# A hybrid S5 / RWKV-7 / Hawk trunk on one core: two weight strips of the first projection in turns, and VectorE's first tile of x ahead of the S5 parameters

## The chip, the core and the metric

The kernel runs on one core of a Trainium2 chip. The metric is the device time of one execution in microseconds (us). Five engines of the core matter here: PE (TensorE, the matmuls), ACT (ScalarE), DVE (VectorE), POOL (GpSimd) and SP (SyncE, which starts most transfers). Each runs its own list of instructions in the order in which the program was built, and waits on semaphores for what the others produce. That order is fixed when the kernel is built; nothing is reordered on the chip.

## The reference

There is one sequence of 256 tokens of width 2048, and two layers, each a mixer followed by a dense SwiGLU network. The change touches only the first layer's mixer:

```
h = rms_norm(x, g)                       # x * rsqrt(mean(x*x) + eps) * g
p = h @ w_in                             # 2048 -> u (1024), r, k, v (3 x 1024), low-rank columns (288)
u -> S5: dt = exp(log_dt); abar = exp(lam * dt); bb = gamma(abar, lam) * b
     s[t] = abar * s[t-1] + bb @ u[t]    # complex diagonal recurrence, 64 groups x 64 modes
     y = gelu(Re(c @ s) + d * u);  y * sigmoid(y @ w_glu)
r, k, v, low-rank -> RWKV-7: a recurrence over t with a 64 x 64 state per head, 16 heads,
     a norm per head, a bonus and a gate
x = x + rms_norm(concat(y_s5, y_rw) @ w_out, g2)
```

Behind it come the network of layer 0, a Hawk block (gate, convolution, real recurrence) and the network of layer 1. All inputs, weights and outputs are 32-bit floats.

## The kernel before

**Matrix products.** Activations are held transposed, 128 features by 256 tokens to a tile (a k-tile). A weight matrix is cut into strips of up to 512 output columns and a strip into groups g of 256 rows, two k-tiles each. A group goes through three steps: SP fetches it as `raw` (512 KB; a ring of three buffers), ACT writes its rounded part `hi` (line 136), and DVE writes the rest, `lo` = raw - hi (line 112); `hi` and `lo` are rings of three too. x is split in the same way into `hh` (ACT) and `hl` (DVE). PE then computes hi·hh, hi·hl and lo·hh (lines 513, 514 and 515) for each k-tile and each 128 columns: 24 matmuls for a group of 512 columns. These are called strip matmuls below and are counted from the start of the kernel: W192 is the point behind the 192nd.

**Strips.** The list `groups`, filled by `plan(...)`, says in which order groups are fetched; a `Strip` object takes them in that order (`take`, `run`, `go`), and when its last group is through (`done`) its result in PSUM (`psw`) is evacuated. The u projection has two strips of 8 groups: u0 (W1 to W192), then u1 (W193 to W384). Then come the low-rank strip (8 groups of 18 matmuls, to W528) and eight strips for r, k and v (to W1680), two for w_glu (to W1872), and the output projection in two halves (to W2256 and W2640).

**The norm.** The strips run on x·g without the factor rsqrt(mean). Meanwhile ACT squares x (`sqs`), PE sums the squares (`ssq`), DVE works out the root (`rs`), PE spreads it over the partitions (`rstdp`), and the evacuation of each u strip multiplies `psw` by `rstd` on DVE (`normed`). The evacuation `u_evac(s)` then copies the strip into tiles `U`, half on ACT and half on DVE, 16 copies each.

**Side work.** While PE runs strips, generators in named lanes emit the S5 and RWKV work between strip matmuls. The lanes are paced by a clock model at build time (`L.now`, `clk`, `rdy`), which settles where each instruction lands in its engine's list. `params()` (lane "par") is the chain of small DVE operations from `lam` (lambda, log dt) to the powers `apr`/`api` and the matrix `bb`. The S5 block runs in eight entries e of 8 channel groups; for each, POOL and DVE write the tables `wb` and `cb` (via `n`) and the angle `ang`, ACT takes its sine `st` and cosine `ct`, PE transposes (`tp`), forms `kt` and `tm`, multiplies `bu` = U·wts, DVE runs the recurrence (`m`, `bu`, scan, `spr`, `spi`), PE sums `py`, and ACT's gelu writes `yg`. Entries 0 to 3 read U of strip u0, entries 4 to 7 that of u1. The tables have two buffers, `ang` and `kt` one, and entry e is not prepared before entry e-2 has been emitted to its end. RWKV runs over four parts hf: `elem`, `solve(hf)` (31 steps, partly on POOL), `chunks(hf)`, and `norm`, whose last steps (`tp`, `yl`, `gp`, `yrf`, `yrh`, `yrl`) make the input of the second half of the output projection.

**Start.** `some(14)` emits 14 steps of `params()` before anything else of this layer; then u0's first group calls `h_before(0)`, which makes the first group's `hi` and `lo` (`ready(1)`), then `hh` of four k-tiles, then `hl` of four.

## Time and profile before

| what | us |
|---|---|
| time, median of 3 runs | 2435.07 |
| lowest and highest run | 2434.27, 2438.75 |
| the profiled execution's own time | 2434.1 |
| its span (first to last instruction of the profile) | 2432.3 |
| PE busy in the span | 2358.0 |
| the first layer's mixer up to the end of its last strip (W2640) | 551.8 |

The span is what the trace shows; 1.8 us of the execution lie outside it. Matmuls overlap each other, so a matmul "lasts" 0.28 us in the rows and the next one starts 0.12 us later. The stage that the change touches lies in the first 551.8 us; what follows is the same code in both kernels.

### The profile page before, as it was taken

Reading aid. Unit: us, or ns where it says so; the run is one execution under the profiler, and the core shown is the slowest. Engines: PE = TensorE matmul, PEld = TensorE weight load, DVE = VectorE, ACT = ScalarE, POOL = GpSimd, SP = SyncE. Lnnn points to the kernel's source line nnn. Section 1 sums busy time; section 2 is a strip of 40 time slices with the busy share of each in tenths; the row PEclk is TensorE's granted clock in tenths of the full one; section 3 lists DMA queues with packets and bytes.
Section 4 is the critical chain, followed back from the end, with each engine's and each line's share of the span. In section 5 each row is a group of like instructions: output and inputs, shape, how many; then the busy total and the mean of one; then the engine's idle time right before and its main releaser. Section 6 shows DMA issues by size and latency. Waiting matters only on the chain.

```text
span 2432.3 us, 47365 instructions
## 1 busy us (share of the span) xinstructions
PE 2358.0 (97%) x19830; PEld 2313.1 (95%) x19830; DVE 1457.4 (60%) x2002; ACT 1180.8 (49%) x1550; POOL 410.5 (17%) x589
## 2 busy tenths in 40 slices
PE   7888999998999999999999999998999999999997
PEld 7888888998999999999999899998999999999997
DVE  9786667568655544555544877757555544555544
ACT  5566545445444444444443687945444444444443
POOL 4773665515000000000000400014000000000002
PEclk8899999999999999999999999999999999999999
DMA  5222534454555555555554455564555555555553
GB/s 199 65 87 83 157 111 134 122 176 148 182 184 185 185 184 184 185 182 186 182 183 164 156 179 194 173 195 137 185 182 187 182 187 186 183 182 183 185 187 114
DMA packets 127446, 404.21 MB, mean 166 GB/s; under 512 B 26112, under 2 KB 26880, under 8 KB 127104
## 3 DMA queue, kind: packets, MB, share of 16 engines
q1 hardware_dynamic: 126912, 399.61, 50.1%
q8 instruction: 155, 2.54, 0.4%
q0 software_dynamic: 320, 1.58, 0.2%
q14 instruction: 59, 0.48, 0.1%
HBM read 397.98 MB, written 3.15 MB: 165 GB/s over the span
## 4 chain that ended last, share of the span: by engine, by line
PE 74%; DVE 3%; POOL 1%; ACT 1%; issue 1%; POOLq 0%; ACTq 0%; DVEq 0%
PE psw L513 24%; PE psw L515 24%; PE psw L514 24%; DVE lo L112 1%; DVE xl L131 1%; POOL xr L112 1%; ACT hi L136 0%; PE ssq L263 0%; PE warm L263 0%; PE own L515 0%; PE own L514 0%; PE own L513 0%; POOL sqs L112 0%; DVE sqs L112 0%; POOL tg L112 0%
## 5 line engine op out<-in xcount | busy, mean ns | idle before, releaser
L112 DVE TENSOR_TENSOR lo<-raw,hi 128x1024 fp32r<-128x1024 f32 (+1 forms) x760 | 931.6, 1230 | 868.9 <-ACT hi L136 867.2
L136 ACT ACTIVATE hi<-raw 128x1024 fp32r<-128x1024 f32 (+1 forms) x760 | 783.7, 1035 | 931.6 <-PE psw L514 733.1
L514 PE MATMUL psw<-xl,hi 128*128 128x256 f32 x3328 | 943.3, 283 | 15.1 <-DVE xl L131 14.8
L513 PE MATMUL psw<-xh,hi 128*128 128x256 f32 x3328 | 942.5, 283 | 0.9 <-ACT xh L136 0.9
L515 PE MATMUL psw<-xh,lo 128*128 128x256 f32 x3328 | 941.4, 283 | 0.0
L514 PEld LDWEIGHTS psw<-xl,hi 128*128 128x128 f32 x3328 | 635.9, 191 | 19.8 <-DVE xl L131 19.8
L513 PEld LDWEIGHTS psw<-xh,hi 128*128 128x128 f32 x3328 | 635.9, 191 | 1.5 <-ACT xh L136 1.5
L515 PEld LDWEIGHTS psw<-xh,lo 128*128 128x128 f32 x3328 | 636.2, 191 | 0.0
L515 PE MATMUL psw<-hhi,lo 128*128 128x256 f32 x1364 | 384.8, 282 | 0.0
L513 PE MATMUL psw<-hhi,hi 128*128 128x256 f32 x1364 | 384.8, 282 | 0.0
L514 PE MATMUL psw<-hlo,hi 128*128 128x256 f32 x1364 | 384.3, 282 | 0.0
L112 POOL TENSOR_TENSOR sqs<-sqs 128x512 f32<-128x512 f32 x44 | 73.0, 1659 | 1519.2 <-ACT sqs L136 1518.7
L514 PEld LDWEIGHTS psw<-hlo,hi 128*128 128x128 f32 x1364 | 257.9, 189 | 0.0
L513 PEld LDWEIGHTS psw<-hhi,hi 128*128 128x128 f32 x1364 | 257.9, 189 | 0.0
L515 PEld LDWEIGHTS psw<-hhi,lo 128*128 128x128 f32 x1364 | 257.9, 189 | 0.0
L513 PE MATMUL psw<-hh,hi 128*128 128x256 f32 x560 | 173.7, 310 | 4.8 <-ACT hi L136 3.2
L514 PE MATMUL psw<-hl,hi 128*128 128x256 f32 x560 | 164.2, 293 | 5.4 <-DVE hl L131 5.4
L515 PE MATMUL psw<-hh,lo 128*128 128x256 f32 x560 | 164.5, 294 | 4.0 <-DVE lo L112 3.9
L513 PEld LDWEIGHTS psw<-hh,hi 128*128 128x128 f32 x560 | 111.1, 198 | 12.7 <-issue 5.8
L514 PEld LDWEIGHTS psw<-hl,hi 128*128 128x128 f32 x560 | 111.6, 199 | 6.3 <-DVE hl L131 6.0
L515 PEld LDWEIGHTS psw<-hh,lo 128*128 128x128 f32 x560 | 111.3, 199 | 5.7 <-DVE lo L112 5.5
L136 ACT ACTIVATE ga<-ga 128x512 f32<-128x512 f32 x52 | 32.8, 632 | 83.0 <-DVE ga L112 82.9
(424 smaller groups left out, 2719.9 us busy)
## 6 DMA issues: line engine op xcount, KB each, us to landing
raw<-in_w_fg SPq DMA_DIRECT2D x352, 512.0 KB, 3.5
raw<-in_w_fd SPq DMA_DIRECT2D x176, 512.0 KB, 3.5
raw<-in_w_oi SPq DMA_DIRECT2D x64, 512.0 KB, 4.0
raw<-in_w_p SPq DMA_DIRECT2D x64, 384.0 KB, 3.2
raw<-in_w_eo SPq DMA_DIRECT2D x32, 512.0 KB, 3.6
raw<-in_w_oo SPq DMA_DIRECT2D x32, 512.0 KB, 3.7
raw<-in_w_u SPq DMA_DIRECT2D x16, 512.0 KB, 4.4
raw<-in_w_glu SPq DMA_DIRECT2D x8, 512.0 KB, 3.5
```

The lines of the kernel that those rows point to most:

```text
L112: e.tensor_tensor(o, x, y, op=op)
L131: e.scalar_tensor_tensor(o, x, s, y, op0=op0, op1=op1)
L136: S.activation(o, x, f, bias=bias, scale=scale)
L513: TE.matmul(o, hi[:, kk, sl], xh, start=st, stop=False, skip_group_check=True)
L514: TE.matmul(o, hi[:, kk, sl], xl, start=False, stop=False, skip_group_check=True)
L515: TE.matmul(o, lo[:, kk, sl], xh, start=False, stop=en, skip_group_check=True)
```

## The change

Three edits. The 16 groups of the two u strips are planned and run in the order of a table `TURNS`, so that both strips stand open in PSUM at once and a k-tile of x serves both before the next is needed. `some(14)` goes, so that all steps of `params()` are emitted by the lane "par"; and `h_before(0)` makes `hh` and `hl` of the first k-tile before the first weight group is split. `solve(hf)` of hf 2 and 3 starts to be emitted only when `chunks(hf-2)` has been emitted to its end.

```diff
+        def strips_in_turns(a, b):
+            for z, g in TURNS:
+                (a, b)[z].go(g)
...
+        TURNS = [(0, 0), (1, 0), (0, 1), (1, 1), (0, 2), (1, 2), (0, 3), (1, 3), (0, 4), (0, 5), (1, 4),
+                 (0, 6), (1, 5), (0, 7), (1, 6), (1, 7)]
+
+        def plan_two(a, b):
+            for z, g in TURNS:
+                plan(((a, b)[z], range(g, g + 1)))
...
-        plan(*w_u, w_lr, *w_p, *w_glu, *w_eo[0], (w_eo[1][0], range(3)), (w_eo[1][1], range(3)),
+        plan_two(*w_u)
+        plan(w_lr, *w_p, *w_glu, *w_eo[0], (w_eo[1][0], range(3)), (w_eo[1][1], range(3)),
...
-            def some(n):
-                for _ in range(n):
-                    next(par)
...
             keep_warm(10)
-            some(14)
...
                 if g == 0:
+                    h_high(0)
+                    h_low(0)
                     ready(1)
+                    ks = ks[1:]
                 for k in ks:
                     h_high(k)
...
-            vdone, ndone = set(), set()
+            vdone, ndone, cdone = set(), set(), set()
...
-                while "ready" not in H:
+                while "ready" not in H or hf > 1 and hf - 2 not in cdone:
                     yield 0.5
...
                     L.add("gn", norm(hf, c2, yc, ys, vr, rs))
+                cdone.add(hf)
...
-            strip(w_u[0], hx, W4, u_evac(0), mid=(h_before, h_behind, hat.get))
-            strip(w_u[1], hx, W4, u_evac(1))
+            strips_in_turns(Strip(w_u[0], hx, W4, u_evac(0), mid=(h_before, h_behind, hat.get)),
+                            Strip(w_u[1], hx, W4, u_evac(1)))
```

Three places show how this moves instructions. The first is DVE's list at the start of the kernel, before the change, from the first parameter row to the first of x; `en` to `y` are rows of `params()`.

```order
L120 TENSOR_SCALAR en<-lam 128x32
L118 TENSOR_SCALAR en<-en 128x32
...
L120 TENSOR_SCALAR y_144<-y_142 128x32
L120 TENSOR_SCALAR omu<-vec 128x27
...
L112 TENSOR_TENSOR lo<-raw,hi 128x1024
L131 SCALAR_TENSOR_TENSOR hl_120<-x0a,vec,hh_118 128x256 x4
L112 TENSOR_TENSOR lo<-raw,hi 128x1024
```

And the same place after it.

```order
L120 TENSOR_SCALAR omu<-vec 128x27
...
L131 SCALAR_TENSOR_TENSOR hl_120<-x0a,vec,hh_118 128x256
L112 TENSOR_TENSOR lo<-raw,hi 128x1024
L131 SCALAR_TENSOR_TENSOR hl_120<-x0a,vec,hh_118 128x256 x3
L112 TENSOR_TENSOR lo<-raw,hi 128x1024
L120 TENSOR_SCALAR en<-lam 128x32
L118 TENSOR_SCALAR en<-en 128x32
```

The parameters have gone behind the second `lo`, and one `hl` stands ahead of the first. The second place is ACT's list around the first gelu (`yg` of entry 0), before the change; `st` and `ct` are the sine and cosine of entry 1, and the `U` copies are the evacuation of strip u1.

```order
L136 ACTIVATE st<-ang 128x256
L136 ACTIVATE ct<-ang 128x256
L136 ACTIVATE ct<-ct 128x256
L136 ACTIVATE Tm_193<-tm 128x512
L136 ACTIVATE hi<-raw 128x576 x2
L136 ACT_TABLE_LOAD
L136 ACTIVATE yg<-py 32x256 x4
L136 ACTIVATE nn<-ang,cc__106 128x256
L136 ACTIVATE nn<-nn,cc__106 128x256
L136 ACTIVATE U_179<-psw_679 32x128 x4
```

And the same place after it, from the second strip's copies on.

```order
L136 ACTIVATE Tm_157<-tm 128x512
L136 ACTIVATE U_143<-psw_189 32x128 x4
...
L136 ACTIVATE U_146<-psw_189 32x128 x4
L136 ACTIVATE hi<-raw 128x576 x3
L136 ACTIVATE st<-ang 128x256
L136 ACTIVATE ct<-ang 128x256
L136 ACTIVATE ct<-ct 128x256
L136 ACT_TABLE_LOAD
L136 ACTIVATE yg<-py 32x256 x4
```

Strip u1's copies have come ahead of the sines of entry 1, which stood ahead of the first gelu and of those copies before. The third place is PE's list at the end of the RWKV part, where the last normalised tile goes through `tp` and `gp` and the next half of the output projection starts with `psw0` on new `hi`; before the change:

```order
L270 MATMUL tp_6556<-cst_75,yc_6450 128x128 x2
L513 MATMUL psw0_6471<-yrh_6301,hi_6473 128x256
...
L263 MATMUL gp_6567<-sg_221,g2_6284 128x128 x4
L513 MATMUL psw1_6472<-yrh_6301,hi_6473 128x256
...
L515 MATMUL psw1_6472<-yrh_6301,lo_6474 128x256
L263 MATMUL ssq_6601<-ones_76 128x1 x2
L513 MATMUL psw0_6303<-yrh_6301,hi_6516 128x256
```

And after it.

```order
L515 MATMUL psw1_6430<-yrh_6236,lo_6432 128x256
L270 MATMUL tp_6577<-cst_75,yc_6521 128x128 x2
L263 MATMUL gp_6582<-sg_185,g2_6358 128x128 x4
L263 MATMUL ssq_6601<-ones_76 128x1 x2
L513 MATMUL psw0_6238<-yrh_6236,hi_6489 128x256
```

Between `tp` and the strip matmul on the new `hi` there stood 21 strip matmuls (6 up to `gp`, 15 behind it); now there is none. In strip matmuls, the first `py` (entry 0) moves from W372 to W420, the second from W414 to W462, the third from W510 to W546, and the eighth stays at W888; `tp` of the last RWKV tile moves from W2379 to W2400.

## Rows read from the trace of the kernel before

**Rows 1.** The page, part 1: busy us (share of the span), instructions, by engine

```profile
PE 2358.0 (97%) x19830; PEld 2313.1 (95%) x19830; DVE 1457.4 (60%) x2002; ACT 1180.8 (49%) x1550; POOL 410.5 (17%) x589
```

**Rows 2.** Waits of PE in 0 to 552 us: waiter, releaser: total, times, longest

```profile
PE psw L514 <- DVE hl L131: 5.4, 3, 3.5
PE kt L263 <- POOL cb L112: 5.3, 4, 2.2
...
PE rstdp L263 <- DVE rs L131: 2.9, 1, 2.9
```

**Rows 3.** Windows by stage: length, busy us (instructions) of PE, PEld, DVE, ACT, POOL, PEclk, DMA

```profile
0.00:46.90 46.90, 33.80 (x224) 32.61 (x225) 41.66 (x132) 23.26 (x40) 13.67 (x26) 0.88 0.65 228
46.90:98.30 51.40, 45.05 (x360) 42.40 (x359) 41.09 (x77) 24.41 (x50) 43.85 (x49) 0.87 0.23 70
...
143.00:226.30 83.30, 70.56 (x573) 64.78 (x573) 65.72 (x133) 59.59 (x99) 40.92 (x50) 0.98 0.28 85
...
300.00:551.80 251.80, 248.99 (x2354) 227.84 (x2354) 162.66 (x335) 124.83 (x214) 116.10 (x241) 1.00 0.44 138
```

**Rows 4.** Windows, one stretch of low granted clock, same columns

```profile
46.20:49.60 3.40, 3.40 (x16) 3.40 (x17) 3.40 (x5) 0.39 (x1) 3.32 (x4) 0.51 0.00 0
```

**Rows 5.** Timeline of ACT at the start: start, length, operation [idle before, releaser]

```profile
6.06 1.06 ACT L136 ACTIVATE hi<-raw 128x1024 fp32r<-128x1024 f32 x1 [3.83 <-DMA raw<-in_w_u]
7.03 1.87 ACT L136 ACTIVATE hh<-x0a,vec 128x256 fp32r<-128x256 f32 x4
```

**Rows 6.** Timeline of DVE at the start

```profile
2.50 3.98 DVE L120 TENSOR_SCALAR en<-lam 128x32 f32<-128x32 f32 x1 [1.37 <-DMA lam<-in_s5lam]
...
9.81 1.22 DVE L112 TENSOR_TENSOR lo<-raw,hi 128x1024 fp32r<-128x1024 f32 x1
...
10.95 1.67 DVE L131 SCALAR_TENSOR_TENSOR hl<-x0a,vec,hh 128x256 fp32r<-128x256 f32 x4
```

**Rows 7.** Timeline of PE in strip u0

```profile
11.48 0.58 PE L514 MATMUL psw<-hl,hi 128*128 128x256 f32 x1 [3.53 <-DVE hl L131]
...
42.85 0.28 PE L514 MATMUL psw<-hl,hi 128*128 128x256 f32 x1
42.97 0.28 PE L515 MATMUL psw<-hh,lo 128*128 128x256 f32 x1
```

**Rows 8.** Timeline of DVE: first row of one entry's recurrence, and strip u1's scaling

```profile
91.91 0.75 DVE L112 TENSOR_TENSOR m<-st,bu 128x256 f32<-128x256 f32 x2 [3.62 <-PE bu L263]
...
98.25 1.29 DVE L112 TENSOR_TENSOR psw<-psw,rstd 128x512 f32<-128x512 f32 x2
```

**Rows 9.** Timeline of PE: first `py` of entries 0 and 7

```profile
86.95 0.33 PE L263 MATMUL py<-U,Tm 128*128 128x64 f32 x2
...
226.28 0.33 PE L263 MATMUL py<-U,Tm 128*128 128x64 f32 x2
```

**Rows 10.** Timeline of ACT from 80 to 112 us

```profile
80.36 0.40 ACT L136 ACTIVATE st<-ang 128x256 f32<-128x256 f32 x1
...
98.98 4.46 ACT L136 ACTIVATE U<-psw 32x128 f32<-32x128 f32 x16 [5.88 <-DVE psw L112]
...
109.85 1.28 ACT L136 ACT_TABLE_LOAD   x1
111.14 0.42 ACT L136 ACTIVATE st<-ang 128x256 f32<-128x256 f32 x1
```

**Rows 11.** Timeline of POOL from 81 to 95 us: entry 2's angle and last table

```profile
81.20 0.61 POOL L112 TENSOR_TENSOR ang<-cst,y 128x256 f32<-128x256 f32 x1 [1.96 <-ACT ct L136]
...
93.01 1.80 POOL L112 TENSOR_TENSOR cb<-n,n 64x320 f32<-64x320 f32 x2
```

**Rows 12.** Timeline of PE at the end of the RWKV part

```profile
523.82 0.38 PE L270 MATMUL tp<-cst,yc 128*128 128x128 f32 x2
...
524.75 1.63 PE L263 MATMUL gp<-sg,g 128*128 128x128 f32 x8
```

**Rows 13.** Timeline of DVE at the end of the RWKV part

```profile
527.56 0.76 DVE L112 TENSOR_TENSOR yrl<-yrf,yrh 128x256 fp32r<-128x256 f32 x2 [0.48 <-ACT yrh L136]
```

## The prediction

> **What bounds the kernel now.** The page's first part is read first: PE is busy 97% of the span, DVE 60%, ACT 49%, POOL 17% [rows 1]. PE sets the time, so a change can only shorten it where PE idles or runs slowly. The windows by stage show where that is: in the last 252 us of the mixer PE is idle for 2.8 us (251.80 less 248.99), but in 0 to 46.9 us for 13.1, in 46.9 to 98.3 for 6.35, and in 143 to 226.3 for 12.7 [rows 3]. The waits of PE name the releasers: `hl` 5.4 us in three waits, `cb` from POOL 5.3 in four, the root of the norm 2.9 in one [rows 2]. A second loss comes on top: after the 2.9 us wait, from 46.2 to 49.6 us, the granted clock is 0.51, that is the 1.2 GHz level, though PE is busy in all of it [rows 4]. At 0.51, 3.4 us do the work of about 1.7, so such a wait costs its own length and 1.7 more. Other long waits of this stage are followed by such a stretch too; I call the 1.7 a clock tax.
>
> At full clock a strip matmul follows the last after 0.12 us [rows 7]. Strip u0's 192 would need 23.0 us and take from 7.6 to 43.3: the strip is paced by its input.
>
> **The change part by part.**
>
> *Start.* Before, DVE begins with parameters: `en` at 2.50 holds it for 3.98 us (waiting within the instruction), and the first `lo` starts only at 9.81, the first `hl` at 10.95 [rows 6], though `hi` is done at 6.06+1.06 = 7.12 [rows 5]. PE waits 3.53 us for `hl` until 11.48 [rows 7]. After, ACT does one `hh` first (1.87/4 = 0.47 us), then `hi` (1.06), and DVE one `hl` (1.67/4 = 0.42), then `lo` (1.22). `hh` shows no wait for x at 7.03, so x is there by then; if it is there at 6.8, `hh` ends at 7.3, `hi` at 8.3, `lo` at 9.6. Before, the first `lo` matmul had its `lo` at 11.03 and ran behind `hl` at 11.86. So PE gets going about 2 us earlier. Bounds: 1.0 us if x lands late enough that `hh` starts at 8, and 3.5 if the whole wait goes. I take 2.0. The parameters now go behind the second `lo`. They have cover as long as `bb`, which the tables of entry 0 need, is not late. If that cover goes, they cost what DVE spent on them ahead of `lo`, 9.81 less 6.5 (where `en` ends) = 3.3 us [rows 6].
>
> *Turns.* A group of x tiles now serves 48 matmuls (5.76 us) instead of 24 (2.88 us), so x is wanted at half the rate. The waits for `hl` after the first (5.4 - 3.5 = 1.9 us, [rows 2]) lose their cause, and the 2.9 for the root too, since PE now has strip matmuls to run while DVE works the root out. That is 4.8 us, with two clock taxes 8.2. Against it stands the supply of weights: the strip's 16 groups must still be fetched and split, with x's tiles on the same two engines, and DVE is busy 41.66 of 46.9 us [rows 3]. Walking ACT, DVE and PE by the durations above, W192 is done near 35 instead of 43.3, but PE waits about 2.3 us for `lo` of group 11 (DVE is in the chain of the root then) and about 3.3 for `kt`, because `cb` of entry 0 is done only near 57.4. Strip u0 is complete at W336 instead of W192. Its evacuation, 1.29 us for both halves of `psw` [rows 8] and some 4.5 of copies (as ACT's, [rows 10]), starts at about 67, and two `lo` come next on DVE. Then `bu`, the recurrence (91.91 to 98.25, 6.3 us of DVE, [rows 8]) and `py` of entry 0 at 82 to 84 us, at W420. Before, it was at 86.95 [rows 9], at W372. The walk's times are estimates, added up from these durations. So PE is ahead by 48 × 0.12 = 5.8 us of strip work and about 4 us of time: a lead of 9.7 us. That is the gross gain of both edits together, the start's 2.0 in it.
>
> *What the lead runs into.* By the two orders of ACT, the sines of entry 1 stand before the first gelu and before u1's copies; afterwards they stand behind u1's copies (4.46 us, [rows 10]) and three `hi`. Before, `st` of entry 1 began at 80.36 [rows 10]; by the walk it begins at about 91. POOL's `ang` of entry 2 has one buffer and follows those sines (81.20 before, released by ACT's `ct`, [rows 11]): about 91.5. From there to the end of the last `cb` POOL took 94.8 - 81.2 = 13.6 us before [rows 11]. In the walk DVE takes some of these rows, and they end at about 102 instead of 94.8. PE, ahead of before, then waits for `kt` of entry 2 some 6 us, after another 5.6 for `lo` of the low-rank strip, which stands behind u1's evacuation on DVE. The lead at the second `py` is then about 3.4 us. After that DVE and POOL are ahead, since u1's evacuation is past, and the old waits of 143 to 226 us (12.7 us, [rows 3]) shrink; but between the first and the eighth `py` there are 468 strip matmuls instead of 516, 5.8 us less of cover. Carrying this through entry 7 I get a lead of 4 to 10 us at its `py` (226.28 before, [rows 9], same place W888). I take 7.0. Its low end is the second `py`'s lead; its high end the whole 9.7.
>
> *Three more table loads on ACT.* One is 1.28 us and the next activation starts 0.01 us after it [rows 10]. All three are 3.8 us of ACT, which is half idle, and one of them lies on the path to a gelu; it is inside the 7.0. The Trainium skill (ScalarE: Activation LUTs, What ACT_TABLE_LOAD costs) gives about 1283 ns for the load and 1380 ns of drain with it, 2.66 us for every switch to another set. By that, the three would be 8.0 us of ACT, and the sum up to 4.1 us worse if all three lay on the path, about no change in all. The trace agrees with the load and shows no drain behind it.
>
> *The gate on `solve`.* It moves solves 2 and 3 later; `qp` of part 3 goes from W1818 to W1938. In 300 to 551.8 us PE idles 2.8 us in all, so there is little to win, and POOL (116 of 252 us) and DVE (163) have room [rows 3]. The loss is at the end: `tp` of the last tile moves to W2400, and the strip matmul behind it needs its result. From `tp` at 523.82 [rows 12] to the end of `yrl` at 527.56+0.76 = 528.32 [rows 13] is 4.5 us. Before, 21 strip matmuls (2.5 us) and `gp` (about 1.55 us net, [rows 12]) covered all but nothing of it; now `gp` and `ssq` (about 2.3 us with their own fill) are the cover. 2.2 us of PE idle are left, plus 0.5 if `tp` itself comes late. Bounds: 0.5 if the chain is faster without strips beside it, and 5.0 with a late `yc` and a clock tax. I take 2.0.
>
> *Sum.* 7.0 won, 2.0 lost: 5.0 us off the profiled execution's 2434.1 is 2429.1. Its time is 1.0 below the median of the runs, which would give 2430.1; I say 2429.6. From the ends (3.4 won and 5.0 lost; 9.7 won and 0.5 lost): 1.6 us slower to 9.2 us faster, and a clock tax more or less at three places is 5 us either way: 2420 to 2440.
>
> **The rivals.**
>
> *The side chains take the lead back* (2435). The entries are made one after the other: `ang`, tables, `kt`, `bu`, recurrence. Where their chain is what PE waits for, being early at W420 only means waiting longer. For it: the `cb` and `kt` waits of the stage [rows 2], and the late sines. Against it: DVE is idle 10 of 51 us and 17.6 of 83 in two of the stages that follow [rows 3], so the chain isn't solid. A switch of ACT's table that held it longer than its row would lead to the same place: at twice 1.28 us [rows 10] three switches are 3.8 us later, 2433.4. The 0.01 us in [rows 10] speaks against it; it has 0.03 of this rival's chance. Otherwise the lead at entry 7 is 2 and the end costs 2: no change. The drain that the Trainium skill tells of (ScalarE: Activation LUTs, What ACT_TABLE_LOAD costs) would be such a longer hold.
>
> *Slower* (2441). One mechanism: with the sines of e1 behind u1's copies the two-deep tables lose one step of lead, and every entry up to 7 has its tables late; PE idles 12 us more from 85 to 226 and pays the tax at two places more. That is 9.7 - 12 - 3.4 - 2 = 7.7 us slower. It decides when entry 7's `py` comes later than 226.3. Against it: the fault is a single delay of about 10 us, and POOL has 42 of 83 us free [rows 3].
>
> *The lead is kept* (2424). The low-rank strip, at W385 to W528, is enough cover for the tables, and one or two clock taxes fall away: 9.7 + 1.7 won, 1.0 lost, from 2434.1.
>
> *The change doesn't do what it says.* Input, not order, paces strip u0, so turns only move the wait from x to weights: then only the start's 2.0 remain and the end eats it, 2434 to 2435. It is counted with the first rival.
>
> **How the numbers follow.** Forecast (2425.5 to 2433) 0.42; lead taken back or nothing done 0.25; lead kept or better 0.18; slower 0.15. A measurement of this kernel can tell 0.2%, 4.9 us, from no change, so faster is below 2430.2. Of the forecast's share somewhat over half lies there (0.26), of the kept lead's nearly all (0.18), together with a little luck in the clock 0.46. The same: the other half of the forecast, the first rival and the mild end of the slower one, 0.38. Slower than 2439.9: 0.16 with the chance that two of the late waits fall together. The range 2418 to 2440 leaves out the worst of the slower case and the best of the kept lead.
>
> **What would show it.** The first `lo` matmul of PE near 9.7 instead of 11.86; no wait for `hl` in 20 to 40 us; no wait for `rstdp`; the first `py` at 82 to 84; a new wait of PE for `kt` near 96 to 102 with `st` of entry 1 near 91; the eighth `py` near 219; a wait for `yrh` of about 2 us right behind the last `tp`; no difference after W2640 but a shift. The forecast is wrong if the eighth `py` stands after 225 or before 216, or if the end costs over 5 us.

## The result: 0.9% slower

| | us |
|---|---|
| after, median of 4 runs (lowest, highest) | 2457.06 (2455.04, 2458.59) |
| before, median of 4 runs beside them | 2436.91 (2434.27, 2439.12) |
| ratio, 95% interval | 1.0088 [1.0076, 1.0100] |
| forecast, range | 2429.6, 2418 to 2440 |

The change costs 21.4 us (0.0088 of 2435), where 5 were to be won. In the profiled executions the span grows from 2432.3 to 2453.2 us and the mixer (up to W2640) from 557.23 to 578.59; the 20.9 and the 21.4 say that all of it lies in the mixer. (The time table has 551.8 for the mixer before, and the prediction calls 300 to 551.8 its last 252 us. In the trace the last strip matmul, W2640, starts at 557.23; PE is not idle in between, so no sum hangs on it.) The page's first part after the change answers to [rows 1]:

```profile
PE 2373.2 (97%) x19830; PEld 2327.2 (95%) x19830; DVE 1453.0 (59%) x2002; ACT 1187.6 (48%) x1553; POOL 406.2 (17%) x589
```

PE has as many instructions and is busy 15.2 us more, 2373.2 for 2358.0: most of the loss doesn't show as idle time but as the same work at a lower clock. The windows by stage show where; the cuts are the first `py` of entry 0 and of entry 7, the last `gp`, W2640 and the end (columns as in [rows 3]). Before:

```profile
0.00:86.95 86.95, 67.60 (x477) 64.57 (x477) 75.33 (x192) 43.78 (x84) 46.92 (x61) 0.86 0.46 158
86.95:226.28 139.33, 121.53 (x994) 112.59 (x993) 108.41 (x220) 95.27 (x172) 84.89 (x106) 0.95 0.25 77
226.28:524.75 298.47, 293.86 (x2719) 268.45 (x2718) 186.77 (x394) 151.10 (x266) 147.62 (x320) 0.99 0.43 128
524.75:557.23 32.48, 32.48 (x269) 32.00 (x267) 24.35 (x23) 15.42 (x22) 11.87 (x7) 1.00 0.77 262
557.23:2432.30 1875.07, 1842.52 (x15381) 1835.45 (x15379) 1062.56 (x1177) 875.18 (x1008) 119.16 (x96) 1.00 0.54 178
```

After:

```profile
0.00:88.10 88.10, 72.19 (x524) 68.08 (x525) 72.74 (x189) 42.52 (x80) 40.88 (x54) 0.90 0.47 163
88.10:236.07 147.97, 124.88 (x944) 116.47 (x943) 103.71 (x214) 97.11 (x172) 88.05 (x109) 0.85 0.23 68
236.07:544.61 308.54, 298.64 (x2737) 272.62 (x2736) 194.38 (x402) 156.50 (x272) 148.54 (x323) 0.98 0.43 127
544.61:578.59 33.98, 33.89 (x254) 33.15 (x252) 19.92 (x23) 16.08 (x22) 9.22 (x7) 0.90 0.66 234
578.59:2453.20 1874.61, 1843.61 (x15381) 1836.87 (x15379) 1062.25 (x1176) 875.35 (x1008) 119.50 (x96) 1.00 0.54 177
```

Length less busy is PE's idle time; busy time times (1 - PEclk) is an estimate of what the low clock costs. In the first stage the changed kernel is better: idle 15.9 for 19.4, and 524 PE instructions are done for 477. From entry 0's to entry 7's `py` it does 50 fewer than before, is idle 23.1 for 17.8 us, and loses 18.7 to the clock (124.88 × 0.15) for 6.1. In the RWKV stage it is idle 9.9 for 4.6 and loses about 6 for 3. At the end 3.4 go to the clock and nothing before. What follows the mixer is unchanged (1874.61 and 1875.07).

The start did what was forecast. The first rows on DVE after the change, to be held against [rows 6]:

```profile
7.23 0.48 DVE L131 SCALAR_TENSOR_TENSOR hl<-x0a,vec,hh 128x256 fp32r<-128x256 f32 x1 [0.70 <-ACT hh L136]
8.18 1.23 DVE L112 TENSOR_TENSOR lo<-raw,hi 128x1024 fp32r<-128x1024 f32 x1 [0.46 <-ACT hi L136]
```

`lo` is done at 9.41 instead of 11.03, and PE's first `lo` matmul starts at 9.46 instead of 11.86 (forecast 9.7; [rows 7] has the wait that went). W192 is done at 36.3 (walked: 35; before 43.0), W264 at 47.0 for 61.5. So the lead is there, over 14 us of it in strip matmuls. Then comes the place that the prediction named. ACT after, to be held against [rows 10]:

```profile
90.30 4.47 ACT L136 ACTIVATE U<-psw 32x128 f32<-32x128 f32 x16 [6.75 <-DVE psw L112]
94.79 1.83 ACT L136 ACTIVATE hi<-raw 128x576 fp32r<-128x576 f32 x3
96.53 0.40 ACT L136 ACTIVATE st<-ang 128x256 f32<-128x256 f32 x1
...
97.70 1.28 ACT L136 ACT_TABLE_LOAD   x1
99.00 2.53 ACT L136 ACTIVATE yg<-py 32x256 f32<-32x256 f32 x4
```

and POOL after, to be held against [rows 11]:

```profile
97.37 0.93 POOL L112 TENSOR_TENSOR ang<-cst,y 128x256 f32<-128x256 f32 x1 [17.95 <-ACT ct L136]
...
106.60 2.19 POOL L112 TENSOR_TENSOR cb<-n,n 64x320 f32<-64x320 f32 x2
```

Entry 1's sine starts at 96.53 (walked: 91; before 80.36), behind u1's copies and three `hi`. POOL stands still for 17.95 us, and entry 2's last `cb` is ready at 108.8 instead of 94.8. PE after, to be held against [rows 9]:

```profile
88.10 0.33 PE L263 MATMUL py<-U,Tm 128*128 128x64 f32 x2
...
95.53 0.58 PE L513 MATMUL psw<-hh,hi 128*128 128x256 f32 x1 [4.49 <-ACT hi L136]
...
105.08 0.42 PE L263 MATMUL kt<-wb,cb 128*32 128x128 f32 x8 [1.03 <-POOL cb L112]
108.85 0.43 PE L263 MATMUL kt<-wb,cb 128*32 128x128 f32 x8 [3.34 <-POOL cb L112]
113.66 0.33 PE L263 MATMUL py<-U,Tm 128*128 128x64 f32 x2
...
236.07 0.33 PE L263 MATMUL py<-U,Tm 128*128 128x64 f32 x2
```

The second `py` comes at 113.66 instead of 98.48 and the eighth at 236.07 instead of 226.28, at the same W888. PE's waits from 0 to 575 us, as in [rows 2], have another leader:

```profile
PE kt L263 <- POOL cb L112: 13.4, 7, 4.5
PE psw L513 <- ACT hi L136: 6.5, 3, 4.5
PE psw L515 <- DVE lo L112: 5.9, 6, 2.0
```

`cb` costs 13.4 us for 5.3. Before, the largest was one that [rows 2] leaves out, RWKV's `bp`:

```profile
PE bp L263 <- DVE av L131: 5.8, 3, 3.5
```

It matters for the mark that this document uses, the eighth `py`. In the kernel before, `bp` stands right ahead of it in PE's list and waits for `av`, 3.4 us beyond the point where the recurrence of entry 7 has made its last tile, `spi`:

```profile
221.96 0.42 DVE L112 TENSOR_TENSOR spi<-bu,m 128x252 f32<-128x252 f32 x1
225.75 0.70 PE L263 MATMUL bp<-av,cst 128*128 128x256 f32 x2 [3.46 <-DVE av L131]
```

After the change no `bp` is in the way, and the eighth `py`, begun at 236.07, waits for `spi` itself:

```profile
237.18 0.42 DVE L112 TENSOR_TENSOR spi<-bu,m 128x252 f32<-128x252 f32 x1
```

So the S5 part ends at 237.6 instead of 222.4, 15.2 us later, where the eighth `py` shows 9.8. The first RWKV product behind it, `qp` of part 0, starts 12.1 us later (244.08 for 232.00).

At the end of the RWKV part, to be held against [rows 12]:

```profile
544.36 0.41 PE L270 MATMUL tp<-cst,yc 128*128 128x128 f32 x2 [1.88 <-DVE yc L112]
544.61 1.63 PE L263 MATMUL gp<-sg,g 128*128 128x128 f32 x8
546.17 1.01 PE L263 MATMUL ssq<-ones 128*128 128x1 f32 x4
547.26 0.58 PE L513 MATMUL psw<-yrh,hi 128*128 128x256 f32 x1
```

`tp` waits 1.88 us for `yc`; behind it the chain to `yrl` (done at 548.0, [rows 13]) leaves PE hardly idle, but the first strip matmuls run at 0.58 and 0.41 us: the low clock again.

### The profile page after: what moved, and what is told of

The parts are those of the page before. It is cut to its first block, busy times and chain, and to the rows that moved or that the text cites. A ratio compares the mean times of both kernels' runs of the same rounds, so it can differ in the third digit from the quotient of the medians.

```text
span 2453.2 us, 47360 instructions
## 1 busy us (share of the span) xinstructions
PE 2373.2 (97%) x19830; PEld 2327.2 (95%) x19830; DVE 1453.0 (59%) x2002; ACT 1187.6 (48%) x1553; POOL 406.2 (17%) x589
## 4 chain that ended last, share of the span: by engine, by line
PE 85%; DVE 7%; ACT 3%; POOL 3%; issue 1%; DMA 1%; SPq 0%; POOLq 0%; ACTq 0%; DVEq 0%
PE psw L513 27%; PE psw L514 26%; PE psw L515 26%; DVE lo L112 2%; DVE xl L131 1%; ACT hi L136 1%; POOL n L112 1%; PE yp L263 1%; DMA raw<-in_w_u 1%; POOL wb L112 1%; PE gp L263 0%; DVE bu L112 0%; POOL cb L112 0%; PE qp L263 0%; PE bu L263 0%
## 5 line engine op out<-in xcount | busy, mean ns | idle before, releaser
L513 PEld LDWEIGHTS psw<-hh,hi 128*128 128x128 f32 x560 | 113.7, 203 | 14.9 <-issue 6.7
L514 PEld LDWEIGHTS psw<-hl,hi 128*128 128x128 f32 x560 | 113.7, 203 | 2.8 <-DVE hl L131 2.5
```

The lines of the kernel that those rows point to most:

```text
L513: TE.matmul(o, hi[:, kk, sl], xh, start=st, stop=False, skip_group_check=True)
L514: TE.matmul(o, hi[:, kk, sl], xl, start=False, stop=False, skip_group_check=True)
```

## The experiments

Ratios are to the kernel before on the same chip, with the 95% interval; 0.001 is 2.4 us. What is read from a trace is one execution: experiments 16 and 17 have the same lists up to W2640, and their traces differ by 4.7 us at the last `gp` and at W2640, so a difference of a few us between two traces there may be chance. "e0" to "e7" are the S5 entries.

**1. The gate alone.** u strips one after the other and the start as before, only the new condition on `solve`.

```diff
-                while "ready" not in H:
+                while "ready" not in H or hf > 1 and hf - 2 not in cdone:
```

> The kernel before with the gate on solve alone (solve of part 2 and 3 emitted after chunks of part 0 and 1); the S5 part keeps its order. Theory A (the gate carries a good part of the loss, because it puts the last tp at W2400 with nothing behind it): PE waits about 2 us for yc at tp and about as long for yrh after gp, each followed by a stretch at half clock; 5 to 9 us slower than before. Theory B (the loss is all in the interleaved strips and the S5 entries; the gate only shifts work): within 2 us of before. The prediction had 2.0 for it.

1.0006 [0.9997, 1.0016]. Its last `tp` stands at W2400 as after the change, and comes at 525.2 us; PE then waits 0.5 us for `yrh`. Theory B: the gate by itself is not the loss, nor is the place at W2400.

**2. Without the new start.** The changed kernel with 14 parameter steps ahead and `ready(1)` ahead of x.

```diff
+            for _ in range(14):
+                next(par)
...
-                    h_high(0)
-                    h_low(0)
                     ready(1)
-                    ks = ks[1:]
```

> The changed kernel with the start of before (14 steps of the parameters ahead of everything, first weight group split before x); turns and gate stay. From W306 on PE's list is that of the changed kernel. Theory A (the start's 2.4 us are swallowed by the waits for cb that come after): same time as the changed kernel within 2 us. Theory B (the early start carries through, or parameters late on DVE make the tables late): 2 to 4 us slower than the changed kernel in the first case, 3 or more faster in the second.

1.0086 [1.0071, 1.0101], the same as the change. The first `lo` matmul is 2.4 us later and the eighth `py` 0.8 us earlier. Theory A: the start is worth nothing here, and turns and gate without it bring the whole loss.

**3. Without the turns.** The changed kernel with u0, then u1.

```diff
-        plan_two(*w_u)
-        plan(w_lr, *w_p, ...
+        plan(*w_u, w_lr, *w_p, ...
...
-            strips_in_turns(Strip(w_u[0], ...), Strip(w_u[1], ...))
+            strip(w_u[0], hx, W4, u_evac(0), mid=(h_before, h_behind, hat.get))
+            strip(w_u[1], hx, W4, u_evac(1))
```

> The changed kernel with the two u strips one after the other as before; the start and the gate stay. Theory A (turns are what makes the S5 entries late: one 10 us step at the second strip's evacuation, then six waits with half clock): this one is at most as slow as the gate alone, 2 to 9 us slower than before, and the eighth py is not later than in before at the same count of strip matmuls. Theory B (parameters emitted late by the lane make tables late and every entry after): most of the loss stays, 12 us or more slower than before.

1.0194 [1.0171, 1.0217]: 47 us, more than with turns. Theory A fell: a loss of this size doesn't need turns. But this kernel has yet another plan: `py` at W378, 438, 480, 564, 636, 675, 762, 834 instead of 372, 414, 510, 552, 672, 711, 816, 888. Theory B's size fits, yet experiment 2 (parameters early, same loss) speaks against its mechanism as the whole: POOL begins its half of `bb` at 48.23 us, 4.6 later than before, which is a part of 47 at most. A third came up (F): what the planner makes of the order, that is, where the entries stand in PE's list, decides.

**4. PE kept busy in the waits for tables.** Matmuls on constants before and between the two halves of `kt`, into columns that nobody reads.

```diff
+                    filler(ps[:, 256:384], {0: 8, 2: 5, 3: 1, 4: 4, 6: 9}.get(e, 0), True)
                     for z in range(2):
+                        if z == 1:
+                            filler(ps[:, 256:384], {0: 6, 2: 14, 3: 6, 4: 20}.get(e, 0), ...)
```

> The changed kernel with matmuls on constants put on PE where it waits at kt for the tables, about as many as fit the waits (14 for entry 0, 19 for entry 2, 7 for 3, 24 for 4, 9 for 6; 73 in all, about 0.2 us each at full clock); their results are not read. Nothing else moves. Theory A (two thirds of the loss is the half clock that follows the waits, not the waits): PE's clock stays up around 62 to 72, 109 to 113, 122 to 126, 143 to 154 and 180 to 188 us, and 5 to 13 us come back. Theory B (tables set the pace; a faster PE only waits longer at the next table): within 2 us of the changed kernel, or slower by what the fillers overrun.

1.0090 [1.0075, 1.0105]. The windows from the first to the eighth `py` and to the last `gp`:

```profile
89.91:237.98 148.07, 132.18 (x1062) 124.06 (x1061) 103.33 (x211) 96.99 (x172) 87.45 (x109) 0.92 0.23 68
237.98:551.22 313.24, 301.76 (x2737) 276.03 (x2735) 195.09 (x402) 156.39 (x272) 146.40 (x323) 0.97 0.43 125
```

The granted clock of the stretch rises from 0.85 to 0.92, and it is as long as without the fillers (148.07 for 147.97). By the estimate above PE is idle 7.2 us less there and loses 8.1 us less to the clock (132.18 × 0.08 = 10.6), and the fillers take some 14 us. The tables come no earlier: entry 2's last `cb` is done at 109.24 (108.79 with the change), entry 7's at 214.78 (214.26). New waits for `cb` stand where there was none or a short one (1.83 us at 76.46, 1.94 at 167.77). So theory A fell for this stage: the low clock is a companion of the waits there, not what sets the time. One flaw: at entry 4 the fillers ran 2.9 us past the `cb` that they were to wait for.

**5 and 6. A second buffer for the angle**, in the changed kernel and in the one before; all lists keep their order.

```diff
-                    ang, nn = sp1("ang", (P, 4, 64)), sp1("nn", (P, 4, 64))
+                    ang, nn = sp1("m2" if e % 2 else "ang", (P, 4, 64)), sp1("nn", (P, 4, 64))
```

> The changed kernel with two buffers for the angle (entries in turn write ang and the space of m2, which is free by then). Every engine's list keeps its order; only POOL's wait for the sine of the entry before goes (17.95 us at 79 to 97 us in the changed kernel). Theory C (the end of the mixer hangs on the side chain S5 entries - RWKV parts, and in the changed kernel this chain lost its 10 us where POOL's tables of entry 2 wait behind the second strip's copies): the wait of PE for kt of entry 2 (4.4 us) goes, the second and third py come 5 to 10 us earlier, and 5 to 12 us of the 21 come back. Theory A (the half clock after waits is the loss): about 2 us back, the clock tax of that one wait. Theory D (turns complete strip u0 30 us later, and this alone sets the chain): no change within 2 us.

> The kernel before with the same two buffers for the angle, order unchanged. Theory C: POOL waits there only 1.96 us for entry 1's sine, so 0 to 3 us faster; if later entries' angles wait as well (4.1 us each at 112 and 120), up to 6. Theory A: no change.

After: 1.0074 [1.0057, 1.0092]; before: 0.9996 [0.9986, 1.0006]. In the changed kernel POOL's rows now read

```profile
80.05 0.61 POOL L112 TENSOR_TENSOR ang<-cst,y 128x256 f32<-128x256 f32 x1
86.71 0.62 POOL L112 TENSOR_TENSOR d<-cst,y 128x256 f32<-128x256 f32 x1 [6.05 <-PE psw L515]
...
95.19 1.77 POOL L112 TENSOR_TENSOR cb<-n,n 64x320 f32<-64x320 f32 x2
```

Entry 2's tables are ready at 97 instead of 109, the third `py` comes 5.4 us earlier (128.54), the eighth 3.3 (232.79). The time is 3.4 us less, which the intervals don't tell apart, and in the trace W2640 is no earlier (580.25 for 578.59). So the late sine makes the S5 part some 3 us late; that it costs time at the end is not shown, and theory C's 5 to 12 us did not come. In the kernel before the time doesn't change.

**7. A delay on POOL, in the kernel before**, ahead of entry 2's angle.

```diff
+                    if e == 2:
+                        scr = sp1("m3", (P, 16, 16))
+                        for _ in range(16):
+                            G.tensor_tensor(scr.rearrange("p a b -> p (a b)"), C["cm"], C["cm"], op=MUL)
                     tt(G, ang, bc(C["io"], 1, 4), bc(th4[:, sl], 2, 64), MUL)
```

> The kernel before with 16 multiplications of constants (about 10 us in all) on POOL ahead of the angle of entry 2; their result is not read, nothing else moves. Theory C: entry 2's tables and all later entries come about 8 to 10 us later, qp of every RWKV part too, and the mixer ends 7 to 11 us later. Theory E (PE's strip work sets the end and side work has slack, as the forecast took it): within 3 us of before.

1.0022 [1.0005, 1.0039], 5.4 us. The delay is 12.83 us long:

```profile
78.52 12.83 POOL L910 TENSOR_TENSOR m<-cst 128x256 f32<-128x256 f32 x16
91.31 0.61 POOL L112 TENSOR_TENSOR ang<-cst,y 128x256 f32<-128x256 f32 x1
```

The eighth `py` comes 7.3 us later (233.61), `qp` of part 0 8.1 later, the last `gp` 9.8 later (534.55), the mixer's end 9.8. The medians beside each other (2442.79 and 2436.95) are 5.8 us apart, so the 9.8 of two single traces holds some chance. Theory C: a delay on POOL, 17% busy, reaches the end of a kernel whose PE is 97% busy. Theory E, the forecast's own premise, has the trace against it; by the times alone its 3 us lie still inside the interval (1.2 to 9.5).

**8. Entry 1's sines ahead of u1's copies**, by holding the evacuation of u1 back.

```diff
                 def f(ps):
+                    while s == 1 and len(tdone) < 2:
+                        L.step()
...
                         tb[e] = yield from tables(e)
+                        tdone.append(e)
```

> The changed kernel with the evacuation of strip u1 emitted only after entry 1's sines. The planner's clock moves with it, so entries 1 to 7 also stand earlier in PE's list (second py at W438 instead of 462, eighth at W834 instead of 888). Theory C: the tables of entry 2 start near 90 instead of 97, and the time improves by 4 to 10 us on the changed kernel. Theory F (entries that stand earlier in PE's list than their tables are ready cost more waits than the earlier sine gives, as in the variant with strips one after the other): the same as the changed kernel or up to 25 us slower.

1.0176 [1.0150, 1.0203], 21 us over the changed kernel. Entry 1's sine begins at 90.13 instead of 96.53. The second `py` comes at 111.3 instead of 113.7 us, and still the eighth at 243.6, at W834: from the second on, `py` stands at W438, 480, 564, 636, 675, 762, 834, the list of experiment 3, with the same kind of loss, although that one has no turns. Theory F.

**9 and 10. One table of turns, two plans.** u0 gets three groups for each of u1; with the new start, and with the old.

```diff
-        TURNS = [(0, 0), (1, 0), (0, 1), (1, 1), (0, 2), (1, 2), (0, 3), (1, 3), (0, 4), (0, 5), (1, 4), ...]
+        TURNS = [(0, 0), (1, 0), (0, 1), (0, 2), (1, 1), (0, 3), (0, 4), (0, 5), (1, 2), (0, 6), (0, 7)] + ...
```

> The changed kernel with another table of turns: u0 gets three groups for each of u1 (u0 complete at W264 instead of W336). In this order entry 1's sines stand ahead of strip u1's copies on ACT, and from W672 on PE's list is that of the gate alone (second py at W438, fourth at W582, eighth at W888, last tp at W2400). Theory F (the turns are harmless by themselves; what costs is the planned list that follows from them: late sines of entry 1, entries whose tables are not ready where PE's list has them): the time of before, 6 us slower at most, perhaps 2 to 4 faster through the start. Theory D (interleaving itself, strip u0's result later): 10 us or more slower than before.

> The same table of turns as in the variant with u0 ahead, but with the start of before (parameters first). Its plan snaps to another list: from W618 on PE's list is nearly that of the changed kernel (fourth py W618, eighth W888, RWKV parts at W912, 1299, 1590, 1938). Theory F: slow like the changed kernel, 12 to 25 us over before, though the turns are those of the other variant and the start is that of before. Theory D or a cost of the start: between before and the other variant, within 4 us of it.

With the new start, whose plan ends like the gate's: 1.0030 [1.0019, 1.0040]. With the old, whose plan ends like the changed kernel's: 1.0083 [1.0068, 1.0098]. The same turns cost 7 us under one plan and 20 under the other. That speaks for theory F against D for the larger part; the 7 us lie a little over F's 6 and under D's 10, so some cost of the turns themselves stays open. The stages of the better one, cut as above:

```profile
0.00:86.25 86.25, 67.17 (x489) 63.83 (x490) 72.25 (x190) 43.09 (x83) 46.66 (x62) 0.88 0.49 163
86.25:228.13 141.88, 118.54 (x982) 110.57 (x981) 110.85 (x226) 102.65 (x177) 82.64 (x102) 0.94 0.25 73
```

It is 9.9 us ahead of the kernel before at W528 and 0.8 ahead at W663. Its `py` of entries 3 to 5 come at 141.5, 161.4 and 179.7 us (138.1, 162.2 and 178.4 before): a lead of ten, and none of these entries more than 0.8 us earlier.

**11. Floors for the places of `kt` and `py`**, so that PE runs strips instead of waiting.

```diff
+                    while wcount[0] < [306, 376, 460, 511, 598, 655, 760, 868][e]:
+                        yield 0.3
                     ps = yield from get("kt")
...
+                    while wcount[0] < [440, 485, 580, 622, 742, 781, 886, 958][e]:
+                        yield 0.3
                     py = yield from get("py")
```

> The changed kernel with a floor for the place of kt and py of each entry in PE's list (entry 0 to 7: py from W440, 485, 580, 622, 742, 781, 886, 958), so that PE runs strips where it waited for tables. The RWKV parts move back as well (last hp W2277 instead of 2232, the last two tiles both at W2400). Theory C (the side chain S5 - RWKV ends last): the waits of PE for cb up to 200 us go, the eighth py is no later than in the changed kernel (236 us) though 90 strip matmuls further on, and what is won is given back at W2400, where PE then waits 5 to 15 us for the last tile; in all within 6 us of the changed kernel. Theory A (waits and the half clock behind them are the loss): 10 to 20 us faster than the changed kernel.

1.0165 [1.0150, 1.0180], 19 us worse than the change. Theory A fell a second time. C's forecast failed as well, within 6 us of the change and the eighth `py` by 236: it came at 261.9, at W978, behind its floor of W958, and the last `gp` at 564.9, behind a wait of 4.22 us for `yc`. So here the S5 part could not be put off for nothing; the RWKV parts came later with it.

**12. Turns of one group**, with the old start.

```diff
+        TURNS = [(0, 0), (1, 0)] + [(0, g) for g in range(1, 8)] + [(1, g) for g in range(1, 8)]
```

> The changed kernel with the start of before and a table in which only one group of u1 is taken early (u0: g0, then u1: g0, then the rest of u0, then of u1); from W672 on the list of the gate alone. Theory F: the time of before, within 4 us. Theory D: 3 to 6 us slower than before, since u0 is complete 24 matmuls later.

1.0009 [1.0000, 1.0019], 2.2 us: theory F, with a plan like the gate's, though the interval doesn't exclude D's 3.

**13 to 15. Lighter tables.** In `cmul` the second product is left out and the first used twice; the planner still counts both, so that the lists stay. With the gate alone (control), with the turns of experiment 9, and with the change.

```diff
                     for z, ap, x in ((m[0], apw[0], u), (m[1], apw[1], v)):
-                        tt(pick(64 * ns), z[:, :, 0:ns], bc(ap[:, sl, s0:s0 + ns], 3, 16), bc(x, 2, ns), MUL)
+                        if z is m[0]:
+                            tt(pick(64 * ns), z[:, :, 0:ns], bc(ap[:, sl, s0:s0 + ns], 3, 16), bc(x, 2, ns), MUL)
...
+                        e_.tensor_tensor(o_, m[0][r, :, 0:ns], m[0][r, :, 0:ns], op=op)
```

> The kernel with the gate alone, with the S5 tables' second product (n from api) left out and the first used twice, so wb and cb are not the reference's; about a quarter of POOL's and DVE's work on the tables goes (some 1.5 us for each of four tables of an entry). Every list keeps its order. Control for the two others. Theory C (the tables' chain sets when py of each entry comes): the waits for cb shrink, 2 to 8 us faster than the gate alone. Theory G (only the order of the list matters, not how long tables take): within 2 us of the gate alone.

> The variant with u0 ahead in turns, with the same part of the tables left out, list unchanged. There PE was 9.9 us ahead of before at W528 and 0.8 at W663. Theory C: with shorter tables part of this lead lives on; 8 us or more faster than that variant with full tables, and faster than the gate alone with the same tables left out. Theory G: no change by itself, and still 4 to 8 us slower than the gate alone.

> The changed kernel with the same part of the tables left out, list unchanged. It waited 13.4 us for cb. Theory C: 8 to 15 us faster than the changed kernel, the eighth py before 229 instead of 236. Theory G (its list, with entry 1's sines behind u1's copies and packed entries, costs by its order alone): within 4 us of the changed kernel.

Control: 0.9995 [0.9982, 1.0008], 2.7 us less than with full tables. Turns of experiment 9: 0.9996 [0.9987, 1.0005], 8.3 us less. The change: 1.0036 [1.0023, 1.0049], 12.7 us less. The kernels in which PE is early gain three to five times as much from lighter tables as the one in which it isn't, whose 2.7 us are not clear of the intervals. Of the 20 us between the change and the gate alone 10 go with a quarter of the tables' work, so this work is a good part of what takes the lead away, and 10 us stay. Theory G fell for the two. The changed kernel's stages then are

```profile
0.00:83.02 83.02, 69.48 (x524) 65.69 (x525) 70.65 (x186) 42.50 (x80) 34.53 (x48) 0.98 0.51 173
83.02:222.56 139.54, 122.02 (x944) 114.67 (x943) 98.69 (x214) 96.88 (x172) 61.07 (x86) 0.88 0.24 72
222.56:534.83 312.27, 301.02 (x2736) 274.39 (x2735) 194.05 (x402) 156.44 (x272) 148.65 (x323) 0.97 0.44 126
```

The eighth `py` is at 222.6, 3.7 us earlier than in the kernel before, but the recurrence that it needs ends at 224.1, 1.7 later than there, and the mixer ends 11.7 us later (568.9): the RWKV stage keeps a loss of its own, idle 11.3 us for 4.6. In the control the recurrence of entry 7 ends 6.8 us earlier than with full tables (216.1 for 222.8), and the last `gp` comes only 1.1 earlier (524.3 for 525.5). Experiment 7's delay was passed on to the end; this lead was not. Of C's forecast for the turns, that they would beat the control, nothing came: 2436.0 and 2435.4 us.

**16 and 17. Another planner's pace in the RWKV stage** of the changed kernel: to the very end, and up to W2640 only.

```diff
-                        L.now += 0.327
+                        L.now += 0.36 if s5over and wcount[0] <= 2640 else 0.327
```

(Experiment 16 without the bound on `wcount`.)

> The changed kernel with the planner's clock for three strip matmuls at 0.36 us instead of 0.327 from the end of the last S5 entry on. The S5 part of the list stays; the RWKV parts move forward in PE's list (qp W1245, 1548, 1851 instead of 1299, 1590, 1938; last gp W2355 instead of 2400). Theory H (in the RWKV stage the list's spacing makes the loss, since PE reached those places late but without waits): the last gp comes 5 to 9 us earlier and 5 to 10 us come back. Theory C (the chain on the other engines is what is late): the last gp comes at the same time within 2 us, PE waits more on the way, and the time is within 3 us of the changed kernel or slower.

> The planner's pace of 0.36 us again, but only from the last S5 entry to the end of the mixer (W2640), so that the stages after it keep the list of the changed kernel. In the run with that pace to the very end the mixer was 5.3 us shorter than in the changed kernel and the rest 4.2 longer. Theory H (in the RWKV stage the list's spacing makes part of the loss): the last gp 5 to 9 us earlier, the mixer 4 to 7 us shorter, the time 3 to 7 us below the changed kernel. Theory C (only the chain of the other engines counts there): within 2 us of the changed kernel.

1.0094 [1.0076, 1.0112] and 1.0075 [1.0061, 1.0089]. In both the RWKV parts stand up to 87 strip matmuls earlier. The last `gp` comes at 537.2 in the first and at 541.9 in the second (544.6 with the change), and the mixer ends at 573.3 and 578.0 (578.6); since the lists are the same up to there, the two differ by chance. Behind the mixer the first is 4.2 us longer than the change and the second 2.0. The time is not less than with the change by more than the intervals tell apart, so theory H's gain is not shown by either.

**18. A try to beat both**: experiment 12 with the pace of 0.34.

> The variant with one early group of u1 (time of before within 0.2%), with the planner's pace at 0.34 us from the last S5 entry to the end of the mixer; the last gp stands at W2358 instead of 2400, with 42 strip matmuls behind it. Try at a version that beats both. Theory H: the RWKV chain ends 2 to 5 us earlier and the wait at W2401 goes: 2434 to 2437, at most 2 us better than before. Theory C: no change against that variant.

1.0049 [1.0035, 1.0062], 10 us worse than experiment 12, which neither theory had; why is not shown. No variant beat the kernel before.

## Why the prediction was wrong

*The start* (2.0 us): right, 2.4 us at the first `lo` matmul, and worth nothing in the end (experiment 2).

*The turns' lead* (9.7 us at the first `py`): half. `py` of entry 0 came at 88.10 instead of 82 to 84, at W420 as forecast; that leaves 5.8 - 1.15 = 4.6 us. The walk had `cb` of entry 0 done near 57.4, 7 us earlier than before, and PE waiting 3.3 us for it. Its last rows, before (on POOL) and after (on DVE):

```profile
62.47 1.79 POOL L112 TENSOR_TENSOR cb<-n,n 64x320 f32<-64x320 f32 x2
61.79 0.98 DVE L112 TENSOR_TENSOR cb<-n,n 64x320 f32<-64x320 f32 x2
```

It was done at 62.8, 1.5 us earlier than before, and PE, which came to `kt` late as well, waited 3.5 us in two waits. Behind them comes a stretch that the walk doesn't name, though the prediction itself had called such a stretch a clock tax: from 61.2 to 72.2 us the clock is 0.53,

```profile
61.20:72.20 11.00, 8.85 (x52) 8.07 (x48) 8.14 (x15) 3.65 (x7) 6.81 (x8) 0.53 0.09 28
```

which costs about 4.2 us (8.85 × 0.47). The walk is on record only by a few of its times, so how the missing five divide between the late `cb` and the low clock is not shown.

*What the lead runs into* (7.0 us left at the eighth `py`): this step failed. Measured: 9.8 us late. Its mechanism at entry 2 was right and undersized (sine at 96.5 for 91, tables at 108.8 for 102), and that wait by itself is only some 3 us (experiment 5). The fault lies in the sentence after it, that DVE and POOL are then ahead and the old waits shrink. It took idle shares (DVE 17.6 of 83 us free) for slack. The entries are a chain: tables on POOL and DVE, `kt`, `bu`, recurrence, `py`, gelu, and the next. Its first links did not come earlier. All tables are made from `bb`. POOL's half of it waits for DVE's half, and starts 1.1 us later than before (first row before, second after):

```profile
43.60 2.46 POOL L112 TENSOR_TENSOR m<-y,bb 128x256 f32<-128x256 f32 x4 [18.82 <-DVE bb L112]
44.71 2.49 POOL L112 TENSOR_TENSOR m<-y,bb 128x256 f32<-128x256 f32 x4 [16.86 <-DVE bb L112]
```

and `bu` of entry 0 starts when it did before, after the change behind the late evacuation of strip u0 (`U`), though PE was 14 us ahead at W264:

```profile
76.48 2.23 PE L263 MATMUL bu<-U,wts 128*128 128x64 f32 x16
76.85 1.97 PE L263 MATMUL bu<-U,wts 128*128 128x64 f32 x16 [0.40 <-DVE U L148]
```

A chain that doesn't start earlier doesn't end earlier. Experiment 7 shows that it passes a delay on, and 13 to 15 that the work on its tables takes a good part of PE's lead.

*The RWKV stage*, for which the sum has nothing but the 2.0 us at its end, is a second term that failed: from the first `qp` to the last `gp` it takes 300.5 us for 292.8, 7.8 more, and the end up to W2640 another 1.5 with 15 strip matmuls fewer. With the 12.1 us up to that `qp` this is the whole loss.

*The rival "slower"* (2441, chance 0.15) named the right place and the right test, the eighth `py` after 226.3. Its price was 12 us of idle time and two taxes; in that stage there were 5.3 us more idle time and about 12.6 more of low clock (18.7 less 6.1), and the RWKV stage and the end took another 12 (idle 5.3, clock about 3 and 3.4), which no rival had.

*Table loads*: the row stays right, the switch at 97.70 holds ACT 1.28 us and `yg` starts at 99.00. The drain that the Trainium skill gives (ScalarE: Activation LUTs, What ACT_TABLE_LOAD costs) is not seen here either.

*The gate* (2.0 us lost): alone 1.5 us, with 0 inside its interval. The forecast wait for `yrh` of 2 us was 0.09 at 547.26 (0.5 in experiment 1); what came was 1.88 for `yc`, which the prediction had only as a bound.

*Range and chances*: the slow end of the sum took 5 us for the end and 3.4 won before it; that the lead could turn negative was left to the rival, and cut off the range.

Shown: that the gate alone costs 1.5 us or nothing (1); that turns and gate bring the whole loss without the new start (2), yet the start without turns loses more (3), and other tables of turns lose 2 to 20 us, the same one 7 or 20 (9, 10, 12), so the loss follows the plan that comes of an edit and not the edit; that a quarter less work on the S5 tables gives back about half of the 20 us over the gate alone (13 to 15); and that filling PE's waits buys nothing (4). Not shown: which feature of the plan makes the larger part, beyond the sine's 3 us in the S5 part; and why the RWKV stage is longer. Its length goes with its list: from the first `qp` to the last `gp` it took 300.4 to 304.7 us in the six traces with the changed kernel's places for it (the change, 2, 4, 5, 10, 15), whatever the S5 part before it did, 295.2 to 299.1 in the five with the gate's (1, 9, 12, 13, 14), 292.8 to 294.4 with those of before (before, 6, 7), and 292.7 and 296.9 under the pace of 0.36 (16, 17), whose times were no better.

## What to carry to other kernels

An engine that is 97% busy can still be paced by one that is 17% busy, if the side work is a chain on which the end hangs; a delay on the chain then costs (experiment 7), while a lead on it may bring little (13). So ask of each microsecond won on the busy engine whether the chain's first link starts earlier. Where a planner fixes the order of every engine, a change moves the whole plan; compare the places of the side work in the list and expect jumps, since the same turns cost 7 or 20 us by the plan that they fell into. Price a wait with the low clock that follows it, and don't count filling it as a gain.

## What the runs showed that was not expected

- The change added more low clock than waiting: from the first to the eighth `py` about 12.6 us more at a mean granted clock of 0.85, against 5.3 us more idle time; and yet raising the clock to 0.92 left the stretch at 148 us (experiment 4).
- Sixteen multiplications of 128x256 in a row took POOL 12.83 us, 0.80 each, where single ones took 0.61 to 0.62 in the rows beside them.
- The kernel came out slower whether the S5 entries stood earlier in PE's list (last `py` at W834: 1.0176 and 1.0194) or later (W978: 1.0165); the kernel before, at W888, sits between them, and so does the change (1.0088), so the place of the last entry alone doesn't settle it.
